# Turning the last attention weights and LayerNorm's sums through DRAM instead of on TensorE, with the late weight loads on ScalarE's queue

## The chip, the cores and the metric

The kernel runs on one core of one Trainium2 chip. A core has five engines, each with its own instruction stream: TensorE (PE, matrix products; its weight loads are shown apart as PEld), VectorE (DVE), ScalarE (ACT), GpSimd (POOL) and SyncE (SP, which here only issues DMAs). They wait for one another through semaphores. An engine works its own stream in order, so an instruction that waits holds everything behind it. The metric is the device time of one execution in microseconds, the median of the runs shown. All arithmetic is in float32, and a matrix product of full precision is built from three passes: each operand is split into a high part (type fp32r) and a low part, and high x high, high x low and low x high are summed.

## The reference, cut to what matters

One layer of a decoder block on 512 tokens of 2048 channels:

```python
h = rms_norm(x); proj = h @ w_in          # split into heads of three mixers
out_a = dilated mixture attention          # 8 heads x 64, windows (128,1), (512,4), (2048,16)
out_b = silu(layer_norm(causal_conv(u * sigmoid(gate))))     # 512 channels, 31 taps
out_c = sliding-window attention with sinks                  # 16 query heads, 2 key heads
x = x + concat(out_a, out_b, out_c) @ w_out
x = x + (silu(h2 @ w_gate) * (h2 @ w_up)) @ w_down,  h2 = rms_norm(x)
```

The A mixer gives, per query, softmax weights over the earlier keys, which the kernel computes as one masked softmax over all 512 tokens. LayerNorm of the B mixer takes mean and variance over its 512 channels for each token.

## The kernel before, in words

Activations lie with channels on the 128 partitions and the 512 tokens along the free dimension. A "slot" is one of 73 SBUF tiles of 128x512. Weights come as units of 128x1024: a DMA into a raw buffer (`pump`, L239 to L251), a cast to the high part on ScalarE (`split_up_to`, L295), a subtraction for the low part on VectorE (L269, `wl`, issued through `lows_now`), then 24 matmuls of 512 columns (L328 to L330). Casts run two units ahead.

The order of everything else is written as ticks. A `Ticks` object holds lists of work due at a tick, and the matmul loops call `tick()` after every six matmuls: eight ticks to an input projection (two units), so ticks 0 to 207 lie in the 26 projections after the head of four, and four to a unit in the first half of the output projection, ticks 208 to 271. `T_MEET = 208` is where the two meet. `late_lows` and `cooling` decide when a unit's subtraction and the next load are issued: in the projections a load follows the release of its buffer by one unit, in the output projection it is issued at the start of the next unit, directly behind the subtraction that read its buffer last, and ahead of the cast of the unit after.

An A head (`attention`, `head`) goes through: scores on TensorE in three units (L863, L864); logits scaled by ScalarE (L941); mask and maximum by VectorE (L946); exponentials by ScalarE (L954, tiles `es[0..2]`); then the weights, which have queries on partitions, must be turned so that keys lie on partitions, as ten 128x128 blocks (causal: 4 + 3 + 2 + 1). Eight of the ten go through DRAM. `blocks_turn` (L971) transposes 32x32 blocks on VectorE into a raw buffer of 128x1024, `blocks_leave` (L976) stores it, `blocks_back` (L983) loads it with the blocks put in place by four DMAs, `blocks_high` (L993) and `blocks_low` (L999) split it into high and low. The other two blocks are turned by TensorE in `flip` (L1006: two transposes into a PSUM bank), then split from PSUM by `high` (L1012) and `low` (L1017). `weigh` (L1030, L1031) multiplies the turned weights with the values.

The depthwise convolution runs as 4 x 31 taps on VectorE (L590), one every 1.4 to 1.9 ticks, with a pause from tick 205 to 215. LayerNorm begins at tick 246 (`T_LN` + 2): `ln_sum`, `ln_split` (L608 to L610), `ln_center` (two matmuls with ones, L617 and L618), `ln_square`, `ln_var` and `ln_out`. `ln_var` turns the sum of squares with four TensorE transposes (`transposed_scale`, L486) and reduces along the free dimension; `ln_out` spreads the result over the partitions with four more (`spread_by_tensor`, L480), at tick 260, and multiplies from PSUM (L633).

In the output projection the product of a unit goes to one of two PSUM banks in turn (pool `tiles`), and VectorE empties the bank with the residual addition (`residual`, L1166, tile `xr`) at the next tick. All DMAs but the first four are issued from SP. Each DMA issue also waits until the DMA that used its completion semaphore before has landed; there are eight such semaphores in turn.

Of the kernel before, what the change touches and what calls it, by code (L numbers as in the profile page):

```python
# [33 lines left out]
OUT_ORDER = (list(range(16)), [n + o for n in range(6) for o in (0, 8)] + [6, 7, 14, 15])  # L34

TAP_TICKS = (1.4, 1.5, 1.9, 1.9)
T_LN = 244
T_MEET = 208
T_GLU = 14

# [20 lines left out]
SPLIT_BUFS = 3  # L61
X_AHEAD = 8
SPLIT_AHEAD = 2
WARM = 8


# [55 lines left out]
def kernel(ctx: ExitStack, tc: tile.TileContext, xT, wi, wo, wgu, wd, cst_in, outT):  # L122
# [118 lines left out]
    def pump(limit, most=99, eng=nc.sync):  # L241
        while at["entry"] < len(entries) and len(raws) < limit and entries[at["entry"]][0] not in held and most:
            most -= 1
            buf, key, parts = entries[at["entry"]]
            size = [part.shape[-1] * (part.shape[1] if len(part.shape) == 3 else 1) for part in parts]
            t, o = take(buf, key, sum(size)), 0
            for part, n in zip(parts, size):
                to = t[:, o:o + n]
                eng.dma_start(to.rearrange("p (n f) -> p n f", n=part.shape[1]) if len(part.shape) == 3 else to, part)
                o += n  # L250
            at["entry"] += 1  # L251

# [221 lines left out]

        ticks.after(2, turn)

    def spread_by_tensor(src4, name):
        b = bank(name)
        for i in range(NT):
            nc.tensor.transpose(b[:, i * P:(i + 1) * P], src4[:, i:i + 1].to_broadcast([P, P]), ident)  # L480
        return b

    def transposed_scale(acc, n, name):
        t, v, r = bank(name), small(name + "v"), small(name + "r")
        for i in range(NT):
            nc.tensor.transpose(t[:, i * P:(i + 1) * P], acc[:, i * P:(i + 1) * P], ident)  # L486
        nc.vector.tensor_reduce(v, t.rearrange("p (a b) -> p a b", b=P), axis=mybir.AxisListType.X, op=ALU.add)
        nc.vector.tensor_scalar(v, v, 1.0 / n, EPS, op0=ALU.mult, op1=ALU.add)
        nc.gpsimd.tensor_tensor(r, v, nhalf[:, :NT], op=ALU.pow)
        return r  # L490

    g4 = [bank(f"in{j}") for j in range(HEAD4)]
    h_hl = {}
    late_lows.append(True)
# [130 lines left out]
            add_square(ln["s"], yconv[j], j, "lq")  # L625

    def ln_var():
        ln["r"] = transposed_scale(ln.pop("s"), 512, "lv")

    def ln_out(mix):  # L630
        b = spread_by_tensor(ln["r"], "lrs")
        for j in range(NB):
            nc.vector.tensor_mul(yconv[j], yconv[j], b)  # L633
        for j in range(NB):
            nc.scalar.activation(yconv[j], yconv[j], AF.Silu, bias=col(C_LB + j), scale=col(C_LG + j))
            mix[f"b{j}"] = yconv[j]
# [179 lines left out]
    def attention(kind, box, mix, mi, heads):  # L816
# [34 lines left out]
        def head(h):  # L851
# [104 lines left out]

            ph, pl = {}, {}

            def block(i, j):
                for u, un in enumerate(us):  # L960
                    for ii, k0, n, o in un:
                        if ii == i:
                            f = o + j * P - k0
                            return es[u][:, f:f + P]

            def blocks_turn():
                z = wp.tile([P, 1024], F32, name=f"{name}z{h}", tag=f"raw{TURN_BUFS[0]}", bufs=1)
                to = z.rearrange("p (j b q) -> p b j q", j=4, b=8)
                for u, c, bs in ((0, slice(0, 2), slice(0, 2)), (0, slice(2, 3), slice(4, 5)), (1, slice(0, 2), slice(2, 6, 3)),
                                 (2, slice(0, 2), slice(3, 7, 3)), (2, slice(3, 4), slice(7, 8))):  # L970
                    nc.vector.transpose(to[:, bs], es[u].rearrange("p (b j q) -> p b j q", b=NT, j=4)[:, c])  # L971
                ticks.after(2, blocks_leave, z)

            def blocks_leave(z):
                d = tc.dram_tile([P, 1024], F32, name=f"{name}ed{h}")
                nc.sync.dma_start(d, z)  # L976
                ticks.after(3, blocks_back, d)

            def blocks_back(d):
                turned[0] = 3 - turned[0]  # L980
                t = wp.tile([P, 1024], F32, name=f"{name}et{h}", tag=f"raw{TURN_BUFS[turned[0]]}", bufs=1)
                for j in range(4):
                    nc.sync.dma_start(t[32 * j:32 * j + 32].rearrange("p (i c) -> p i c", i=4),  # L983
                                      d.rearrange("(i p) c -> p i c", i=4)[:, :, j * 2 * P:(j + 1) * 2 * P])
                ticks.after(5, blocks_high, t.rearrange("p (i b q) -> p b i q", i=4, b=8))

            def queries4(t):
                return t.rearrange("p (b i q) -> p b i q", b=NT, i=4)

            def blocks_high(src):  # L990
                for t in range(2):
                    ph[t] = slot(f"{name}ph{h}{t}", F32R)
                    nc.scalar.copy(queries4(ph[t]), src[:, NT * t:NT * t + NT])  # L993
                ticks.after(EV, blocks_low, src)

            def blocks_low(src):
                for t in range(2):
                    pl[t] = slot(f"{name}pl{h}{t}", F32R)
                    nc.vector.tensor_sub(queries4(pl[t]), src[:, NT * t:NT * t + NT], queries4(ph[t]).bitcast(F32))  # L999

            def flip(t):
                b = bank(f"{name}t{h}{t}")
                o = 0
                for j, i0, i1 in TBANKS[kind][t]:
                    for i in range(i0, i1 + 1):
                        nc.tensor.transpose(b[:, o:o + P], block(i, j), ident)  # L1006
                        o += P
                ticks.after(ev, high, t, b, o)

            def high(t, b, o):  # L1010
                ph[t] = slot(f"{name}ph{h}{t}", F32R)
                nc.scalar.copy(ph[t][:, :o], b[:, :o])  # L1012
                ticks.after(EV, low, t, b, o)

            def low(t, b, o):
                pl[t] = slot(f"{name}pl{h}{t}", F32R)
                nc.vector.tensor_sub(pl[t][:, :o], b[:, :o], ph[t][:, :o].bitcast(F32))  # L1017

            def weigh():
                b = bank(f"{name}o{h}")  # L1020
# [41 lines left out]
            if kind == "c":  # L1062
                ticks.after(tu, packed_exps)
                ticks.after(tu + s2, packed_norm)
                ticks.after(tu + 1, packed_turn)
            else:
                ticks.after(tu + s2, invert, h, den)
                ticks.after(tu + 2, blocks_turn)
                ticks.after(tu + s2 + fl + 2, flip, 2)
            ticks.after(t0 + at_v, weigh)  # L1070
            if h == 1:
                ticks.after(t0 + at_v - 2, sums_back)
# [21 lines left out]
    t_tap = T_GLU + 2  # L1094
    for j in range(NB):
        for i in range(TAPS):
            if T_MEET - 3 <= t_tap < T_MEET + 7:
                t_tap = T_MEET + 7
            ticks.after(int(t_tap), tap, j, i)
            t_tap += TAP_TICKS[j]  # L1100
    t_ln = T_LN
# [3 lines left out]
    ticks.after(t_ln + 4, ln_center)  # L1105
    ticks.after(t_ln + 6, ln_square)
    ticks.after(t_ln + 11, ln_var)
    ticks.after(t_ln + 14, ln_out, mix)
    for n, row in enumerate(r for r in ROWS if r[0] == "b"):
        ticks.after(t_ln + 15 + n, split_mix, row)  # L1110

    shared = {}
    cooling.append(True)
# [679 lines left out]
```

## Time and profile before

| | |
|---|---|
| median of 3 runs | 1826.89 us (1826.79 to 1827.04) |
| the profiled execution | 1827.03 us |
| its span, first to last instruction | 1825.3 us |
| TensorE's granted clock | 0.999 |
| busy PE, DVE, ACT, POOL | 100%, 79%, 73%, 56% |
| DMA traffic | 354.61 MB, mean 194 GB/s |

The profile is one execution. A row of the order of time gives the start and duration in us, the engine, the line of the kernel, the operation, output<-inputs with shapes, a count when alike instructions were merged, and in square brackets the idle time of the engine just before with what ended it. Engine names with q (SPq, ACTq) are the sequencer that issues DMAs. The input projections run from about 9 to 376 us, the output projection to about 562 us, and the feed-forward part takes the rest. The A heads of the four tiles a0 to a3 (two heads each) are turned between about 309 and 434 us.

### The profile page before, as it was taken

How to read it: one execution, taken by the hardware profiler on the slowest of the kernel's cores; microseconds unless marked ns; L12 is line 12 of the kernel's file. 1: busy time of each engine (PE TensorE's matmuls, PEld its weight loads, DVE VectorE, ACT ScalarE, POOL GpSimd, SP SyncE). 2: the span in 40 equal slices, each digit the busy share in tenths (PEclk: the TensorE clock that was granted, in tenths of full speed). 3: DMA queues.
4: the chain of work that ended last, by engine and by line, in shares of the span. 5: the costliest groups of instructions: out<-in, count | busy, mean ns of one | idle time of the engine just before them, and what ended most of it. 6: DMA issues, size and time to landing. Idle time of an engine off the chain costs nothing.

```text
span 1825.3 us, 26570 instructions
## 1 busy us (share of the span) xinstructions
PE 1818.3 (100%) x8191; PEld 1509.9 (83%) x8191; DVE 1434.5 (79%) x1996; ACT 1327.6 (73%) x1848; POOL 1022.1 (56%) x793
## 2 busy tenths in 40 slices
PE   9999999999999999999999999999999999999998
PEld 7888888888888888888888888888888888888887
DVE  6779999987689777777777777777777777777777
ACT  6345656664468778888888888888887778877775
POOL 0116555120014577786887868878775568775652
PEclk9999999999999999999999999999999999999999
DMA  7355456666343557787777877778687579877645
GB/s 279 96 161 157 152 172 182 195 211 214 130 145 113 130 142 206 191 222 192 194 205 191 220 192 197 204 190 223 176 278 261 195 230 293 259 256 255 231 127 105
DMA packets 409295, 354.61 MB, mean 194 GB/s; under 512 B 177088, under 2 KB 331840, under 8 KB 409152
## 3 DMA queue, kind: packets, MB, share of 16 engines
q1 hardware_dynamic: 408576, 352.12, 65.7%
q8 instruction: 65, 1.06, 0.2%
q10 hardware_dynamic: 576, 0.79, 0.1%
q14 instruction: 78, 0.64, 0.1%
HBM read 270.00 MB, written 74.41 MB: 189 GB/s over the span
## 4 chain that ended last, share of the span: by engine, by line
PE 99%; DVE 1%; DMA 0%; issue 0%; ACT 0%; SPq 0%; DVEq 0%; ACTq 0%
PE out L1374 15%; PE out L1375 15%; PE out L1372 15%; PE out L1637 7%; PE out L1639 7%; PE out L1638 7%; PE o L328 3%; PE o L330 3%; PE o L329 3%; PE cq L328 2%; PE cq L329 2%; PE cq L330 2%; PE ak L328 1%; PE aq L328 1%; PE av L328 1%; PE ak L330 1%
## 5 line engine op out<-in xcount | busy, mean ns | idle before, releaser
L1372 PE MATMUL out<-wh,h 128*128 128x512 f32 x1232 | 479.2, 389 | 0.0
L1374 PE MATMUL out<-wl,h 128*128 128x512 f32 x1232 | 479.2, 389 | 0.0
L1375 PE MATMUL out<-wh,h 128*128 128x512 f32 x1232 | 479.2, 389 | 0.0
L1372 PEld LDWEIGHTS out<-wh,h 128*128 128x128 f32 x1232 | 231.2, 188 | 48.1
L1374 PEld LDWEIGHTS out<-wl,h 128*128 128x128 f32 x1232 | 231.2, 188 | 48.1
L1375 PEld LDWEIGHTS out<-wh,h 128*128 128x128 f32 x1232 | 231.2, 188 | 47.9
L1637 PE MATMUL out<-wh,a 128*128 128x512 f32 x620 | 240.4, 388 | 0.0
L1638 PE MATMUL out<-wl,a 128*128 128x512 f32 x620 | 240.3, 388 | 0.0
L1639 PE MATMUL out<-wh,a 128*128 128x512 f32 x620 | 240.3, 388 | 0.0
L295 ACT CAST wh<-w 128x1024 fp32r<-128x1024 f32 (+2 forms) x94 | 97.0, 1032 | 115.8 <-PE o L329 48.9
L1647 DVE TENSOR_TENSOR y<-y,out 128x512 f32<-128x512 f32 x192 | 128.6, 684 | 47.6 <-PE out L1639 46.1
L269 DVE TENSOR_TENSOR wl<-w,wh 128x1024 fp32r<-128x1024 f32 (+2 forms) x95 | 114.1, 1203 | 30.0 <-ACT wh L295 28.9
L1639 PEld LDWEIGHTS out<-wh,a 128*128 128x128 f32 x620 | 116.4, 188 | 24.0
L1638 PEld LDWEIGHTS out<-wl,a 128*128 128x128 f32 x620 | 116.4, 188 | 23.8
L1637 PEld LDWEIGHTS out<-wh,a 128*128 128x128 f32 x620 | 116.4, 188 | 23.8
L590 DVE SCALAR_TENSOR_TENSOR y<-bu,cst,y 128x511 f32<-128x511 f32 (+14 forms) x120 | 89.8, 748 | 0.5
L328 PE MATMUL o<-mh_c,wh 128*128 128x512 f32 x128 | 50.3, 393 | 0.0
L328 PE MATMUL cq<-hh,wh 128*128 128x512 f32 x128 | 50.0, 391 | 0.0
L329 PE MATMUL cq<-hl,wh 128*128 128x512 f32 x128 | 49.9, 390 | 0.0
L329 PE MATMUL o<-ml_c,wh 128*128 128x512 f32 x128 | 49.9, 390 | 0.0
L330 PE MATMUL o<-mh_c,wl 128*128 128x512 f32 x128 | 49.9, 390 | 0.0
L330 PE MATMUL cq<-hh,wl 128*128 128x512 f32 x128 | 49.8, 389 | 0.0
(2359 smaller groups left out, 4736.4 us busy)
## 6 DMA issues: line engine op xcount, KB each, us to landing
od<-a SPq DMA_DIRECT2D x154, 256.0 KB
a<-od SPq DMA_DIRECT2D x154, 256.0 KB
w<-in_wi SPq DMA_DIRECT2D x58, 512.0 KB
w<-in_wo SPq DMA_DIRECT2D x32, 512.0 KB
x<-in_xT SPq DMA_DIRECT2D x16, 256.0 KB
xr<-in_xT SPq DMA_DIRECT2D x16, 256.0 KB
x2d<-xr SPq DMA_DIRECT2D x16, 256.0 KB
z<-x2d SPq DMA_DIRECT2D x64, 64.0 KB
```

The source lines that it names most:

```text
L269: fn(*args)
L295: (nc.vector.tensor_copy if u == 0 else nc.scalar.copy)(hi[:, :n], t[:, :n])
L328: nc.tensor.matmul(out, wh, xh, start=start, stop=False)
L329: nc.tensor.matmul(out, wh, xl, start=False, stop=False)
L330: nc.tensor.matmul(out, wl, xh, start=False, stop=stop)
L1372: nc.tensor.matmul(b, x[:, high], wh[:, s], start=c == f == 0 and q in (7, 1, 5, 2), stop=False, skip_group_check=True)
L1374: nc.tensor.matmul(b, x[:, high], wl[:, s], start=False, stop=False, skip_group_check=True)
L1375: nc.tensor.matmul(b, x[:, low], wh[:, s], start=False, stop=c == f == 1, skip_group_check=True)
L1637: nc.tensor.matmul(b[:, lo:hi], x[:, high], wh[:, s], start=start, stop=False, skip_group_check=True)
L1638: nc.tensor.matmul(b[:, lo:hi], x[:, high], wl[:, s], start=False, stop=False, skip_group_check=True)
L1639: nc.tensor.matmul(b[:, lo:hi], x[:, low], wh[:, s], start=False, stop=last, skip_group_check=True)
L1647: getattr(eng, op)(t, t, src)
```

## The change

Five things are done.

1. `flip`, `high`, `low`, `block` and `queries4` go. `blocks_turn` also transposes, on VectorE, the two blocks that `flip` turned, into a second tile `z2` of 128x256 (a slot); `blocks_leave` stores that too (`ec`), `blocks_back` loads it with four more DMAs (`eu`), and `blocks_high` and `blocks_low` split three tiles where they split two, five ticks after the loads are issued.
2. LayerNorm's `transposed_scale` and `spread_by_tensor` go. `ln_var` calls `token_scale` (a reduction with 32x32 transposes on VectorE, four small DMAs to DRAM one tick later, one back two ticks later, additions and a power on GpSimd three ticks later) and `spread` (a transpose on VectorE two ticks later, four small DMAs, then one that broadcasts the row over 128 partitions into a slot). `ln_out` multiplies from that slot.
3. `T_LN` goes from 244 to 231; the steps up to `ln_var` come 13 ticks sooner, `ln_out` comes at tick 259 in place of 260.
4. The taps' pause ends at tick 211 in place of 215.
5. Weight units with a key of 46 or more (the last 17 units of the input projection and the 32 of the output projection) are loaded by DMAs on ScalarE's queue, at the same points of the program.

```diff
-T_LN = 244
+T_LN = 231
...
+ACT_LOADS = 46
...
-                eng.dma_start(to.rearrange("p (n f) -> p n f", n=part.shape[1]) if len(part.shape) == 3 else to, part)
+                by = nc.scalar if isinstance(key, int) and key >= ACT_LOADS else eng
+                by.dma_start(to.rearrange("p (n f) -> p n f", n=part.shape[1]) if len(part.shape) == 3 else to, part)
...
     def ln_var():
-        ln["r"] = transposed_scale(ln.pop("s"), 512, "lv")
+        ln["r"] = slot("lrs")
+        token_scale(ln.pop("s"), 512, "lv", ticks.after, lambda v, r, wide: spread(wide, "l", ln["r"]))
...
     def ln_out(mix):
-        b = spread_by_tensor(ln["r"], "lrs")
         for j in range(NB):
-            nc.vector.tensor_mul(yconv[j], yconv[j], b)
+            nc.vector.tensor_mul(yconv[j], yconv[j], ln["r"])
...
-                ticks.after(2, blocks_leave, z)
+                z2 = slot(f"{name}z{h}", cols=2 * P)
+                to = z2.rearrange("p (j b q) -> p b j q", j=4, b=2)
+                for n in range(2):
+                    nc.vector.transpose(to[:, n], es[n + 1][:, 2 * P:3 * P].rearrange("p (j q) -> p j q", j=4))
+                es.clear()
+                ticks.after(2, blocks_leave, z, z2)
...
+                d2 = tc.dram_tile([P, 2 * P], F32, name=f"{name}ec{h}")
+                nc.sync.dma_start(d2, z2)
...
+                t2 = slot(f"{name}eu{h}", cols=2 * P)
+                for j in range(4):
+                    nc.sync.dma_start(t2[32 * j:32 * j + 32].rearrange("p (i c) -> p i c", i=4),
+                                      d2.rearrange("(i p) c -> p i c", i=4)[:, :, j * 64:(j + 1) * 64])
...
-                ticks.after(tu + s2 + fl + 2, flip, 2)
...
-            if T_MEET - 3 <= t_tap < T_MEET + 7:
-                t_tap = T_MEET + 7
+            if T_MEET - 3 <= t_tap < T_MEET + 3:
+                t_tap = T_MEET + 3
...
-    ticks.after(t_ln + 14, ln_out, mix)
+    ticks.after(t_ln + 26, ln_out, mix)
     for n, row in enumerate(r for r in ROWS if r[0] == "b"):
-        ticks.after(t_ln + 15 + n, split_mix, row)
+        ticks.after(t_ln + 27 + n, split_mix, row)
```

More of the change, by code (lines that the diff above doesn't have):

```diff
@@ L475, in spread @@
         ticks.after(2, turn)
[L477 to L490, printed above, removed]
     g4 = [bank(f"in{j}") for j in range(HEAD4)]
@@ L957, in head @@
             ph, pl = {}, {}
[L959 to L964, printed above, removed]
             def blocks_turn():
@@ L971, in blocks_turn, with blocks_leave, blocks_back @@
                     nc.vector.transpose(to[:, bs], es[u].rearrange("p (b j q) -> p b j q", b=NT, j=4)[:, c])
-                ticks.after(2, blocks_leave, z)
-            def blocks_leave(z):
+                z2 = slot(f"{name}z{h}", cols=2 * P)
[4 more added lines that the diff above has]
+                ticks.after(2, blocks_leave, z, z2)
+            def blocks_leave(z, z2):
                 d = tc.dram_tile([P, 1024], F32, name=f"{name}ed{h}")
                 nc.sync.dma_start(d, z)
-                ticks.after(3, blocks_back, d)
-            def blocks_back(d):
+                d2 = tc.dram_tile([P, 2 * P], F32, name=f"{name}ec{h}")
+                nc.sync.dma_start(d2, z2)
+                ticks.after(3, blocks_back, d, d2)
+            def blocks_back(d, d2):
                 turned[0] = 3 - turned[0]
@@ L984, in blocks_back @@
                                       d.rearrange("(i p) c -> p i c", i=4)[:, :, j * 2 * P:(j + 1) * 2 * P])
[L985 to L991, printed above, removed]
+                t2 = slot(f"{name}eu{h}", cols=2 * P)
+                for j in range(4):
+                    nc.sync.dma_start(t2[32 * j:32 * j + 32].rearrange("p (i c) -> p i c", i=4),
+                                      d2.rearrange("(i p) c -> p i c", i=4)[:, :, j * 64:(j + 1) * 64])
@@ L992, in blocks_high, with by_query @@
+                b8 = t.rearrange("p (i b q) -> p b i q", i=4, b=8)
+                ticks.after(5, blocks_high, (b8[:, :NT], b8[:, NT:], t2.rearrange("p (i b q) -> p b i q", i=4, b=2)))
+            def by_query(t, src):
+                return t[:, :src.shape[1] * P].rearrange("p (b i q) -> p b i q", i=4, q=32)
+            def blocks_high(srcs):
+                for t, src in enumerate(srcs):
                     ph[t] = slot(f"{name}ph{h}{t}", F32R)
-                    nc.scalar.copy(queries4(ph[t]), src[:, NT * t:NT * t + NT])
@@ L994, in blocks_high, with blocks_low @@
-                ticks.after(EV, blocks_low, src)
-            def blocks_low(src):
-                for t in range(2):
+                    nc.scalar.copy(by_query(ph[t], src), src)
+                ticks.after(EV, blocks_low, srcs)
+            def blocks_low(srcs):
+                for t, src in enumerate(srcs):
                     pl[t] = slot(f"{name}pl{h}{t}", F32R)
[L999 to L1017, printed above, removed]
+                    nc.vector.tensor_sub(by_query(pl[t], src), src, by_query(ph[t], src).bitcast(F32))
             def weigh():
```

## The prediction

> **What bounds the kernel now.** I read the page first (the span, the busy shares, the chain that ended last), then TensorE's waits, then the order of time on each engine around the places that the diff names.
>
> ```profile
> span 1825.3 us, 26570 instructions
> ...
> PE 1818.3 (100%) x8191; PEld 1509.9 (83%) x8191; DVE 1434.5 (79%) x1996; ACT 1327.6 (73%) x1848; POOL 1022.1 (56%) x793
> ...
> PE 99%; DVE 1%; DMA 0%; issue 0%; ACT 0%; SPq 0%; DVEq 0%; ACTq 0%
> ```
>
> The waits of TensorE in the whole execution are two, and both lie outside the part that changes (the start and the last product):
>
> ```profile
> PE idle L354 <- DVE nhalf L360: 1.1, 1, 1.1
> PE sides L1602 <- DVE y L1616: 1.1, 2, 0.6
> ```
>
> So TensorE is the bound, and it never stands still between them. Two things can move the time: TensorE's own instructions that go away, and waits of TensorE that do not exist yet. Everything else is slack, and the question is how much of it there is where the change uses it. The 40 slices of the page cannot show that, since an average over 45 us hides a slack of 1 us. The order of time can.
>
> **What TensorE loses.** Each of the 8 A heads has one `flip`, two 128x128 transposes between two 512-wide matmuls. In the order of time on TensorE:
>
> ```profile
> 315.60 0.40 PE L330 MATMUL ak<-hh,wl 128*128 128x512 f32 x1
> 315.83 0.38 PE L1006 MATMUL a0t<-ident,a0e 128*128 128x128 f32 x2
> 315.97 0.47 PE L328 MATMUL ak<-hh,wh 128*128 128x512 f32 x1
> 316.29 0.39 PE L329 MATMUL ak<-hl,wh 128*128 128x512 f32 x1
> ```
>
> From the start of L330 to the start of L329 two matmuls normally pass, each 0.23 us after the other (315.60 to 315.83). That is 0.46 us, and here it is 0.69: the pair costs 0.23. The chain tells the same, and gives the two groups of four that LayerNorm uses (L486, L480):
>
> ```profile
> 316.00 0.22 PE a0t L1006 x2
> ...
> 454.82 0.44 PE lv L486 x4
> ...
> 459.39 0.44 PE lrs L480 x4
> ```
>
> Eight pairs at 0.23 are 1.84 us, LayerNorm's 0.88, in sum 2.7. The matmuls just behind an interruption start up to 0.01 us late for some steps, which may add some tenths; I take 2.8.
>
> One transpose alone is longer than its place in the queue:
>
> ```profile
> L1006 PE MATMUL a0t<-ident,a0e x4: 270/272/273, 315.8 to 328.4; 128*128 128x128 f32 x4
> ```
>
> If each took its whole 0.272 us out of TensorE's time, 24 would give 6.5 us. That is a rival below; the starts above speak against it. [...]
>
> **What takes the place.** Per head VectorE gets two more 128x128 transposes, ScalarE and VectorE keep one copy and one subtraction each (now from SBUF, five ticks later, with the other two), and SyncE's queue (SP) gets one store and four loads. LayerNorm's variance gets ten small DMAs on SP and a few short instructions on VectorE and GpSimd. In 380 to 440, where A heads 2 and 3 run beside the output projection, VectorE is the busy one; in 382 to 388 it is full:
>
> ```profile
> 382.00:388.00 6.00, 6.00 (x31) 5.08 (x30) 5.97 (x14) 4.14 (x12) 0.00 (x0) 1.00 0.19 39
> ...
> 380.00:440.00 60.00, 60.00 (x285) 50.24 (x284) 48.50 (x105) 34.08 (x72) 2.31 (x3) 1.00 0.69 215
> ```
>
> The columns are the window, its length, then PE, PEld, DVE, ACT, POOL busy (count), clock, DMA share, GB/s. So I look at that place step by step. First SP, which runs there without a pause:
>
> ```profile
> 349.43 0.34 SPq L976 DMA_DIRECT2D a1ed<-a1z  x1
> ...
> 351.10 0.60 SPq L249 DMA_DIRECT2D w<-in_wo  x1
> ...
> 358.16 2.02 SPq L983 DMA_DIRECT2D a1et<-a1ed  x4
> ...
> 364.35 0.58 SPq L249 DMA_DIRECT2D w<-in_wo  x1
> 365.11 0.34 SPq L664 DMA_DIRECT2D aq2t<-aq2d  x1
> 365.50 0.43 SPq L249 DMA_DIRECT2D w<-in_wo  x1
> ```
>
> **SP's term.** A head's new store and four loads cost one issue like L976 and four like L983: 0.34 + 2.02 = 2.4 us in front of aq2t. The two weight loads ahead of aq2t leave: 0.60 + 0.58 = 1.2. Net +1.2 from this head. Of the head before it (another 2.4, less its own loads) pauses of SP take part; bounds 0 to 1.2 more, since nothing that I see gives time back. I take aq2t 1.5 us later, between 0 (if the shorter ring makes the transfers land sooner) and 2.4.
>
> **The path from aq2t to TensorE.** It is short of slack at each step:
>
> ```profile
> 374.33 0.82 ACT L941 ACTIVATE a2s<-a2s,aq2r 128x128 f32<-128x128 f32 x2 [4.06 <-POOL aq2r L674]
> ...
> 383.08 1.05 ACT L295 CAST wh<-w 128x1024 fp32r<-128x1024 f32 x1
> ```
>
> ```profile
> 375.72 0.69 DVE L1086 TENSOR_TENSOR ml_c<-mix_c,mh_c 128x512 fp32r<-128x512 f32 x1 [2.92 <-ACT mh_c L1085]
> ...
> 382.03 0.69 DVE L1086 TENSOR_TENSOR ml_a<-mix_a,mh_a 128x512 fp32r<-128x512 f32 x1 [2.29 <-ACT mh_a L1085]
> ...
> 385.12 1.22 DVE L269 TENSOR_TENSOR wl<-w,wh 128x1024 fp32r<-128x1024 f32 x1
> 386.25 0.68 DVE L1166 TENSOR_TENSOR xr<-xr,o 128x512 f32<-128x512 f32 x1
> 386.94 1.45 DVE L971 STREAM_TRANSPOSE a2z<-a2e 128x256 f32<-128x256 f32 x5
> ...
> 389.02 0.73 DVE L590 SCALAR_TENSOR_TENSOR y<-bu,cst,y 128x490 f32<-128x490 f32 x1
> 389.66 1.22 DVE L269 TENSOR_TENSOR wl<-w,wh 128x1024 fp32r<-128x1024 f32 x1
> ...
> 391.91 0.69 DVE L1166 TENSOR_TENSOR xr<-xr,o 128x512 f32<-128x512 f32 x1
> ```
>
> ```profile
> 387.93 0.39 PE L328 MATMUL o<-mh_c,wh 128*128 128x512 f32 x1
> ...
> 393.82 0.39 PE L328 MATMUL o<-mh_c,wh 128*128 128x512 f32 x1
> ```
>
> ScalarE stood 4.06 us waiting for GpSimd's aq2r (which comes from aq2t), VectorE then 2.92 and 2.29 us for ScalarE, and VectorE's xr (L1166, the residual that empties a PSUM bank) ends at 386.93, while TensorE's third unit of the output projection, which writes that bank again (two banks, in turn), starts at 387.93. The slack is 1.0 us; at the next unit it is 393.82 - 392.60 = 1.2.
>
> Into this path the change puts: 1.5 us of SP; two weight loads that ScalarE now issues where the output projection begins; and two taps, since the pause ends four ticks sooner (tick 211 in place of 215, one tap per 1.9 ticks), ahead of xr. A DMA issue on ScalarE's queue is seen once, at the start, four in 1.86 us:
>
> ```profile
> 0.80 1.86 ACTq L249 DMA_DIRECT2D w<-in_wi  x4
> ```
>
> So the loads cost 0.93 together (0 if they hide behind a running instruction), and a tap 0.64 (389.02 to 389.66), two of them 1.3. TensorE itself arrives 4 x 0.23 = 0.9 sooner. Stall at this bank: 1.5 + 0.9 + 1.3 + 0.9 - 1.0 = 3.6 us; from 0 (nothing on SP, issues hidden, transfers sooner) to 4.5 (SP at 2.4).
>
> **The weight loads as waits on ScalarE.** A load into a buffer waits for the `wl` subtraction that read it last. On SP that wait is seen in 376 to 476:
>
> ```profile
> SPq L249 <- DVE wl L269: 29.5, 8, 10.0
> ```
>
> There only DMAs stand behind it. On ScalarE the next unit's cast, the exponentials, the logits and the copies out of PSUM stand behind it, and VectorE waits for those. At the second unit ScalarE is ready at 383.08, and wl ends at 386.34: it would stand 3.3 us. From E, the end of that wl: issue 0.46, cast 1.05, the last exponential and its sum some 0.9, then a2z 1.45 and two new transposes 0.5 (1.45 / 5 each), that is E + 4.4; from there the rows as before, from the end of a2z (388.39) to the end of the second xr (392.60), 4.2: E + 8.6, where it was E + 6.3. This is 2.3 later against a slack of 1.2: a further 1.1, between 0 (if the issue goes out ahead of a running instruction and VectorE has other work) and 2.3. [...]
>
> Seven more of the eight waits follow, at later units. Their bounds are 0 and about 8 us (the 29.5 scaled by the 3.3 us at the second unit against the longest, 10.0, is 9.7, less the 1.1 used). I take 2.5, near the lower end, because ScalarE has 26 of 60 us free in 380 to 440.
>
> **LayerNorm's mean in TensorE's queue.** It moves 13 ticks forward, into the stretch where heads 3 run.
>
> ```profile
> 439.65 0.69 DVE L610 TENSOR_TENSOR lnl<-lns,lnh 128x512 fp32r<-128x512 f32 x1 [2.77 <-ACT lnh L609]
> ```
>
> ```profile
> 443.63 0.39 PE L618 MATMUL lnm<-lnl,one 128*128 128x512 f32 x1
> ```
>
> TensorE's second matmul of the mean starts 3.3 us after the end of lnl (440.34). VectorE and ScalarE some 3 us late use that up: 0 to 2 us, I take 0.5. The two DRAM trips have 15 ticks of 1.4 us (six matmuls); I cost them at nothing. Their cover is that stretch; were it gone, VectorE's multiplications would wait for the broadcast and the `xr` behind them would be late, which the 8 us above hold.
>
> **Sum.** -2.8 + 3.6 + 1.1 + 2.5 + 0.5 = +4.9 us. The profiled execution took 1827.03 us (1.7 outside its span), the median of the runs is 1826.89, so the difference between them is 0.1 and I let it go: 1827.0 + 4.9 = 1832 us, +0.27%. With all upper ends: -2.8 + 4.5 + 2.3 + 8 + 2 = +14.0, 1841. With all costs at 0: 1824.1. A difference under 0.2%, 3.65 us, cannot be told from none.
>
> **Rivals.**
> - **No stall (not slower).** One mechanism: the smaller ring. With the weight loads on the other queue SP's transfers land sooner, aq2t is not late, and ScalarE's long wait at 374.33 shrinks by as much as taps and issues add. It decides at the bank of 387.93: if xr ends no more than 0.1 us later than now (its 1.0 slack less the 0.9 that TensorE comes sooner), there is no wait, and the time is 1827.0 - 2.8 = 1824.2, within 0.2%. For it: ScalarE has waits to give. Against: VectorE has none in 382 to 388.
> - **The stall stays at two banks.** VectorE catches up in 400 to 440. Then -2.8 + 3.6 + 1.1 = +1.9, 1829, within 0.2%.
> - **The transposes cost their whole duration**: 24 x 0.272 = 6.5 without stalls, 1820.5, faster. Against it stand the starts at 315.83 to 316.29. [...]
> - **The waits go whole to ScalarE and on to TensorE**: 29.5 - 2.8, 1854. Against: TensorE has over 1 us in most units.
>
> **How the numbers follow.** The forecast case 0.47 (1830.5 to 1841), no stall 0.25, two banks 0.17, whole durations 0.06, whole waits 0.05. Faster by over 0.2% is 0.06, within 0.25 + 0.17 = 0.42, slower 0.47 + 0.05 = 0.52. The range runs from 1823.8 (no stall, some tenths better) to 1841.5 (the upper ends) and leaves out the two smallest cases.
>
> **What would show it.** Right: no L1006, L486 or L480 on TensorE and 24 fewer matmuls and 24 fewer weight loads; TensorE waits for VectorE's L1166 rows (xr) near 387 and 393, in sum 3 to 9 us; ScalarE waits for wl at its weight loads; aq2t issued 1 to 2 us later on SP. Wrong: no waits of TensorE in 370 to 480 and a span 2.8 shorter (the slack was larger than the bank rows say), or TensorE waits first on a weigh or a score (then SP's lag, not VectorE, decides).

## The result, and the profile after

| | before | after |
|---|---|---|
| median of 4 runs, us | 1826.84 (1826.44 to 1827.04) | 1846.16 (1842.84 to 1848.08) |
| ratio, 95% interval | | 1.0104 (1.0087 to 1.0122) |
| the profiled execution, us | 1827.03 | 1848.08 |
| its span, us | 1825.3 | 1846.4 |

The change makes the kernel 19.3 us slower. The prediction was 1832.0 with a range to 1841.5: the direction was right, the size was not. Line numbers below are those of the kernel after the change where its profile is read (the residual xr is L1139, the cast L297, the weight load L251, the low part wl L271).

The page of after, its head and its chain of waits:

```profile
span 1846.4 us, 26614 instructions
...
PE 1824.0 (99%) x8167; PEld 1512.0 (82%) x8167; DVE 1438.3 (78%) x2013; ACT 1327.0 (72%) x1848; POOL 1026.3 (56%) x796
...
PE 73%; DVE 1%; issue 0%; DMA 0%; ACT 0%; DVEq 0%
```

TensorE has its 24 matmuls fewer (8191 to 8167), and yet more busy time. TensorE's waits in the whole execution (total, times, longest in us):

```profile
PE a2s L850 <- DMA aq<-aq2l: 8.9, 1, 8.9
PE o L330 <- ACT mh_b L1058: 3.0, 1, 3.0
PE o L330 <- DVE xr L1139: 1.8, 3, 1.3
...
PE a1o L1004 <- ACT a1ph L985: 1.0, 1, 1.0
PE lnm L604 <- DVE one L595: 0.6, 1, 0.6
PE a1o L1005 <- DVE a1pl L991: 0.2, 1, 0.2
PE lnm L605 <- DVE lnl L597: 0.2, 1, 0.2
```

Where there were no waits in the changed part, there are 15.7 us now. The largest is the first score of A tile 2 (L850), which waits for a DMA that copies the low part of its queries to the other half of the partitions (aq<-aq2l, issued at L689 and L690). I call these two DMAs the twin copies. The second is put down to mh_b, a row of mixer B, since a cast of such a row was the last thing to end before it. But the matmul that stood there, at 482.30, belongs to the first half of the output projection, which reads rows of mixer C only; the first matmul with mh_b starts at 497.5. VectorE's xr ended 0.15 us before that matmul started, as another did 0.14 us before the one at 407.63, so this wait too is one for xr. With it the waits for xr, which the prediction put first, are 4.8 us, none of them near 387 or 393.

The waits are not all. The stretches with the two long ones, before and then after (window, length, busy PE, PEld, DVE, ACT, POOL with counts, clock, DMA share, GB/s):

```profile
376.00:388.00 12.00, 12.00 (x57) 10.06 (x56) 9.59 (x23) 10.07 (x24) 1.04 (x1) 1.00 0.52 163
476.00:492.00 16.00, 16.00 (x72) 13.24 (x71) 7.66 (x12) 5.53 (x9) 0.00 (x0) 1.00 0.37 131
```

```profile
376.00:388.00 12.00, 8.31 (x29) 7.19 (x30) 6.69 (x11) 5.33 (x11) 4.24 (x3) 0.59 0.83 235
476.00:492.00 16.00, 12.97 (x45) 10.15 (x44) 8.91 (x12) 5.99 (x9) 0.00 (x0) 0.79 0.29 98
```

The granted clock was 1.00 and is 0.59 and 0.79. In the order of time on TensorE, behind the two waits:

```profile
379.69 0.45 PE L850 MATMUL a2s<-ak2h,aq 128*128 128x128 f32 x1 [8.87 <-DMA aq<-aq2l]
...
381.11 0.63 PE L331 MATMUL aq<-hl,wh 128*128 128x512 f32 x1
381.54 0.63 PE L332 MATMUL aq<-hh,wl 128*128 128x512 f32 x1
...
482.30 0.76 PE L330 MATMUL o<-mh_c,wh 128*128 128x512 f32 x1 [3.03 <-ACT mh_b L1058]
...
488.38 0.40 PE L332 MATMUL o<-mh_c,wl 128*128 128x512 f32 x1
```

A step of 512 columns takes 0.43 us there (381.11 to 381.54) in place of 0.23. From 482.30 to 488.38 lie 14 steps, 6.1 us in place of 3.2: 2.9 us lost. From 379.69 to 385.99 TensorE does matmuls of 6912 columns in sum, 6.3 us where 13.5 steps of 0.23 are 3.1: 3.2 lost. So the account of the profiled execution is 15.7 of waits + 6.1 of slow clock - 2.8 of transposes = 19.0; the spans differ by 21.1. Most of the other 2 us lies at the edges of the nine waits. A row's idle time begins at the end of the matmul before, 0.39 us after its start, where without a wait the next one starts after 0.23; so each wait costs 0.16 us more than its row says, 1.4 in sum, and the first step behind a wait is some 0.1 longer than others (0.56 us from 482.30, where the next ones take 0.43).

Why the twin copies are late is seen on SP, after:

```profile
351.07 4.28 SPq L974 DMA_DIRECT2D a1eu<-a1ec  x4
...
370.51 2.38 SPq L970 DMA_DIRECT2D a1et<-a1ed  x4
...
377.26 0.47 SPq L689 DMA_DIRECT2D aq<-aq2l  x1
377.77 0.60 SPq L690 DMA_DIRECT2D aq<-aq2l  x1
378.87 0.34 SPq L651 DMA_DIRECT2D aq2t<-aq2d  x1
```

aq2t was issued at 365.11 before; it is 13.8 us later, where the prediction had 1.5. And why xr is late before 482.30, on VectorE and ScalarE:

```profile
472.60 2.49 DVE L620 TENSOR_TENSOR y<-y,lrs 128x512 f32<-128x512 f32 x4 [2.17 <-DMA lrs<-le]
...
476.17 0.60 ACT L1058 CAST mh_a<-mix_a 128x512 fp32r<-128x512 f32 x1
478.71 0.34 ACTq L251 DMA_DIRECT2D w<-in_wo  x1
479.14 1.04 ACT L297 CAST wh<-w 128x1024 fp32r<-128x1024 f32 x1 [2.37 <-PE o L331]
480.09 2.17 ACT L1058 CAST mh_b<-y 128x512 fp32r<-128x512 f32 x4
...
480.74 0.69 DVE L1059 TENSOR_TENSOR ml_b<-y,mh_b 128x512 fp32r<-128x512 f32 x1 [2.10 <-ACT mh_b L1058]
481.46 0.69 DVE L1139 TENSOR_TENSOR xr<-xr,o 128x512 f32<-128x512 f32 x1
```

VectorE first stands 2.17 us for LayerNorm's broadcast (lrs). ScalarE, free at 476.77, stands in front of the weight load until 478.7, when VectorE's wl has ended (L271, from 477.41, 1.22 long). The cast of the weights behind that load (wh) is put down to a matmul of TensorE that ended at 479.04, as late as the load's issue, so the load is not the only thing in front of it. Then come the casts of the b rows; VectorE stands 2.10 us for the first of them, and xr is behind that.

### The profile page after: what moved, and what is told of

The parts are those of the page before. It is cut to its first block, busy times and chain, and to the rows that moved or that the text cites. A ratio compares the mean times of both kernels' runs of the same rounds, so it can differ in the third digit from the quotient of the medians.

```text
span 1846.4 us, 26614 instructions
## 1 busy us (share of the span) xinstructions
PE 1824.0 (99%) x8167; PEld 1512.0 (82%) x8167; DVE 1438.3 (78%) x2013; ACT 1327.0 (72%) x1848; POOL 1026.3 (56%) x796
## 4 chain that ended last, share of the span: by engine, by line
PE 73%; DVE 1%; issue 0%; DMA 0%; ACT 0%; DVEq 0%
PE out L1347 15%; PE out L1345 15%; PE out L1348 15%; PE out L1610 7%; PE out L1612 7%; PE out L1611 7%; PE o L330 2%; PE o L331 2%; PE o L332 2%; DVE wl L293 0%; DVE y L1620 0%; DMA out_T<-z 0%; DVE z L1519 0%; ACT mh_b L1058 0%; DVE y L1589 0%
## 5 line engine op out<-in xcount | busy, mean ns | idle before, releaser
L297 ACT CAST wh<-w 128x1024 fp32r<-128x1024 f32 (+2 forms) x94 | 96.9, 1031 | 133.9 <-PE o L331 43.7
L271 DVE TENSOR_TENSOR wl<-w,wh 128x1024 fp32r<-128x1024 f32 (+2 forms) x95 | 114.1, 1203 | 28.2 <-ACT wh L297 23.8
```

The lines of the kernel that those rows point to most:

```text
L271: fn(*args)
L297: (nc.vector.tensor_copy if u == 0 else nc.scalar.copy)(hi[:, :n], t[:, :n])
```

## The experiments

The theories were these. **V** is the prediction's: SP a little late, then VectorE and ScalarE too tight at the banks of the first output units. **S**: the added issues on SP. **Q**: the weight loads on ScalarE's queue, whatever else. Later ones are named where they come up. All ratios are against the kernel before, measured beside it on the same chip. "Twin" is the issue of the first aq<-aq2l on SP and TensorE's wait for it, in the profiled execution (363.20 and none before).

| run | ratio, 95% interval | twin issued, wait (us) |
|---|---|---|
| after | 1.0104 (1.0087 to 1.0122) | 377.26, 8.9 |
| e1 loads back on SP | 1.0063 (1.0048 to 1.0078) | 367.78, 2.3 |
| e2 only loads on ScalarE | 1.0081 (1.0065 to 1.0096) | 367.65, 0.9 |
| e3 only the turn | 1.0020 (1.0010 to 1.0029) | 370.95, 2.6 |
| e4 only LayerNorm, taps | 1.0040 (1.0025 to 1.0055) | 361.64, 0 |
| e5 as e4, sums on TensorE | 1.0020 (1.0011 to 1.0029) | 363.36, 0 |
| e6 as e4, 4 ticks sooner | 1.0015 (1.0005 to 1.0024) | 364.43, 0 |
| e7 loads of 46 to 62 only | 1.0000 (0.9990 to 1.0009) | 367.24, 0 |
| e8 as e2, a unit later | 1.0022 (1.0013 to 1.0031) | 368.11, 1.0 |
| e9 LayerNorm at old ticks | 1.0007 (0.9997 to 1.0016) | 360.92, 0 |
| e11 after, a unit later | 1.0072 (1.0055 to 1.0089) | 373.11, 7.6 |
| e12 as e1, 5 loads on ScalarE | 1.0080 (1.0065 to 1.0095) | 372.47, 6.2 |
| e14 as e3, DMAs on GpSimd | 0.9989 (0.9980 to 0.9999) | 362.41, 0 |
| e15 as e1, 5 loads on GpSimd | 1.0076 (1.0061 to 1.0091) | 373.35, 6.8 |
| e16 all, repaired | 0.9993 (0.9984 to 1.0002) | 364.78, 0 |
| e17 e14 again | 0.9991 (0.9982 to 1.0000) | 367.19, 1.0 |
| e18 as e1, 3 loads on GpSimd | 1.0062 (1.0040 to 1.0085) | 370.12, 3.3 |
| e19 as e1, 3 loads on ScalarE | 1.0066 (1.0044 to 1.0089) | 371.10, 5.1 |
| e20 after, turn on GpSimd | 1.0092 (1.0075 to 1.0109) | 368.73, 2.9 |

e14 and e17 are one kernel: its twin came at 362.41 in one execution and at 367.19 in another. A difference of a few us in that column alone proves little; groups of runs do.

### The parts by themselves

e1 undoes the weight loads; e2, e3 and e4 are the kernel before with one part each.

```diff
-ACT_LOADS = 46
+ACT_LOADS = 999
```

> The change with one part undone: the weight loads from unit 46 on are issued by SP again. Theory Q (the loads on ScalarE's queue are the cause: ScalarE stands before each of them, and SP, which shares the eight completion semaphores with it, is held too): the wait of 8.9 us for aq<-aq2l and the slow clock behind it go, and so does most of the wait for mh_b; 1825 to 1831 us. Theory S (the turn's and LayerNorm's extra issues on SP are the cause, whoever issues the loads): SP now has the weight loads as well, so the wait stays or grows; 1840 us or more. Theory V (my prediction's: VectorE and ScalarE too tight at the banks of the first output units): 1828 to 1832, with waits for xr.

> The kernel before with one part of the change alone: weight loads from unit 46 on by ScalarE's queue. Theory Q: most of the loss shows without the rest, 1834 to 1846 us, with ScalarE idle 3 to 6 us ahead of loads in 340 to 390 and SP's aq2t several us later than 365.1. Theory S: within 2 us of the kernel before, 1825 to 1829. Theory V: 1827 to 1831 (0.9 us of issues and waits for wl on ScalarE).

> The kernel before with one part alone: all ten blocks of every A head turned through DRAM (one more store and four more loads per head on SP), the rest as before. Theory Q: TensorE loses 1.8 us of transposes, small waits come; 1824 to 1830 us. Theory S: SP's 2.4 us per head add up (8 heads), aq2 late by 5 us or more, TensorE waits at aq<-aq2l; 1834 us or more. Theory V: 1826 to 1829 (SP 1.5 to 2.4 us later, slack of 1 us at the bank of 387.93).

> The kernel before with one part alone: LayerNorm's variance through DRAM trips with T_LN 231 and the taps' pause ending at 211. All theories of the first loss (Q, S, V): TensorE loses eight transposes (0.9 us), 1825.5 to 1827 us. If the trips themselves make the b rows late (my prediction cost them at nothing): TensorE waits for mh_b by about 3 us, and 1829 to 1833 us.

Measured, in us against 1826.5 of before: e1 1837.98 (+11.5), e2 1841.74 (+15.2), e3 1830.02 (+3.5), e4 1833.41 (+6.9). So no theory of one cause stands: every part costs something alone, and they add up to 25.6, more than the 19.3 of all together. e4, which all three theories had near 1826, is the plainest miss; the reading beside them, that the trips cost, is met in kind (1833.41 against 1829 to 1833), but with a wait for xr and not for mh_b. The profiled execution of e2 is the fastest of its four (1837.97), that of e3 the slowest of its ten (1834.42), so their waits are not those of the medians. TensorE's waits, of e1, e2, e3 and e4:

```profile
PE o L330 <- DVE xr L1139: 7.3, 3, 5.1
PE a2s L850 <- DMA aq<-aq2l: 2.3, 1, 2.3
```

```profile
PE o L330 <- DVE xr L1168: 9.5, 4, 3.6
...
PE a2s L865 <- DMA aq<-aq2l: 0.9, 1, 0.9
```

```profile
PE a2s L863 <- DMA aq<-aq2l: 2.6, 1, 2.6
PE o L328 <- DVE xr L1152: 2.5, 1, 2.5
```

```profile
PE o L328 <- DVE xr L1151: 4.4, 1, 4.4
```

The prediction's waits for xr are there, in e2 above all, where they are 9.5 us.

### The weight loads on ScalarE's queue

ScalarE's idle time in e2, between 376 and 485, by what ended it:

```profile
ACT wh L297 <- DVE wl L271: 22.0, 7, 5.8
ACT wh L297 <- issue: 20.1, 7, 3.6
```

```profile
396.41 0.34 ACTq L251 DMA_DIRECT2D w<-in_wo  x1
396.79 1.05 ACT L297 CAST wh<-w 128x1024 fp32r<-128x1024 f32 x1 [3.29 <-DVE wl L271]
```

42.1 us of ScalarE stand in front of a load, and the cast behind it starts 0.4 us after it is issued. Two runs test whether it is the wait for wl (theory **W**) or the queue as such (theory **C**: ScalarE and SP share eight completion semaphores, in the trace of after 214 DMAs of the two to each). e7 moves only the loads of the projections, which come one unit after their buffer is released; e8 moves all, but issues those of the output projection one unit later.

```diff
+                by = nc.scalar if isinstance(key, int) and ACT_LOADS <= key < 63 else eng
```

```diff
         if late_lows and not cooling:
-            pump(RAW_EARLY if at["use"] <= 20 else RAW_BUFS)
+            n = room(RAW_BUFS) if at["use"] > 2 * N_IN + 1 else 0
+            if n:
+                due.append(n)
...
         at["use"] += 1
+        if due:
+            pump(RAW_BUFS, due.pop())
```

> The kernel before with the weight loads of units 46 to 62 alone on ScalarE's queue (the projections, where a load comes one unit after its buffer is released); the 32 of the output projection stay on SP. Theory W (what costs is a load's wait for the subtraction wl, placed ahead of the next cast): those loads have nothing to wait for, so 1826 to 1829 us. Theory C (the eight completion semaphores that the two queues share hold both, wherever the loads are): ScalarE idle before these loads too, 1832 us or more.

> The run with the loads from 46 on by ScalarE's queue alone, with each load of the output projection issued one unit later in ScalarE's stream, when the subtraction that read its buffer is long done. Theory W: ScalarE's 42 us of waits ahead of casts in 376 to 485 fall under 15, TensorE's waits for xr go; 1826 to 1830 us. Theory C: they stay for the most part, 1835 us or more.

e7: 1826.90, no difference. e8: 1831.21, a little over W's range; of e2's 15.2 us 10.7 are gone, no cast of e8 waits for wl any more, and TensorE's waits for xr fell from 9.5 to 0.6:

```profile
PE a2s L880 <- DMA aq<-aq2l: 1.0, 1, 1.0
PE o L345 <- DVE xr L1183: 0.6, 1, 0.6
```

W is shown, as the larger part of the loads' price. What stays in e8, 4.5 us by the medians, is only 1.6 in waits of its profiled execution (1829.29 us, under the median of its runs), and the twin copies are 4 to 5 us later than before in the profiled executions of e2, e7 and e8 alike, though SP has fewer issues there. W does not explain that.

### LayerNorm

VectorE in e4 at the place of the 4.4 us:

```profile
461.13 2.50 DVE L618 TENSOR_TENSOR y<-y,lrs 128x512 f32<-128x512 f32 x4 [4.35 <-DMA lrs<-le]
...
467.79 0.69 DVE L1151 TENSOR_TENSOR xr<-xr,o 128x512 f32<-128x512 f32 x1
```

It stands 4.35 us for the broadcast (lrs<-le), and the xr that empties TensorE's bank is behind. Theory **T** says that the two DRAM trips are not covered, theory **O** that ln_out at tick 259 and the shorter pause are too tight whatever turns the sums.

> The run with LayerNorm and the taps alone, but its sums again turned on TensorE (eight transposes back): T_LN 231, ln_out at tick 259, the taps' pause to 211. Theory T (the DRAM trips are later than tick 259 lets them be): without them 1825.5 to 1828.5 us, no wait for xr near 468. Theory O (the earlier tick and the shorter pause make VectorE too full where A head 3 is turned, whatever turns the sums): 1832 us or more, the wait near 468 stays.

> The run with LayerNorm and the taps alone, its steps up to the variance four ticks (5.6 us) sooner (T_LN 227), ln_out and the b rows at the same ticks as there. Theory T: the 4.35 us that VectorE stood for the broadcast are covered, TensorE's wait for xr near 468 goes; 1825.5 to 1828 us. Theory O: the wait stays or moves to the mean's two matmuls (lnm); 1831 us or more.

e5 1830.62, e6 1829.25: each lies between the two, so each theory has a part. In e5 a wait of 1.9 us for xr stays near 466 with no trip at all, in e6 one of 2.5; and 0.3 and 0.8 us near 388, where the pause is shorter. e9 takes O's part away and gives the trips three ticks more (18 in place of 15).

```diff
-T_LN = 231
+T_LN = 229
...
-            if T_MEET - 3 <= t_tap < T_MEET + 3:
-                t_tap = T_MEET + 3
+            if T_MEET - 3 <= t_tap < T_MEET + 7:
+                t_tap = T_MEET + 7
...
-    ticks.after(t_ln + 26, ln_out, mix)
+    ticks.after(t_ln + 29, ln_out, mix)
```

> LayerNorm's variance through DRAM alone, with nothing else made tighter: T_LN 229 (two ticks sooner than in the change), ln_out and the b rows at tick 260 and 261 as in the kernel before, the taps' pause to 215 as before. If what the earlier runs showed is all (trips that were not covered; ln_out one tick sooner, ahead of an xr; two taps more ahead of the xr near 388), no wait is left and TensorE is 0.9 us shorter: 1825.5 to 1826.5 us. If the trips as such cost (SP's ten issues): 1828 us or more.

1827.96, between the two ranges and not told apart from before by its interval: the waits near 388 and 466 are gone, but one of 2.7 us has come at 447. VectorE's longest wait in e9 in 430 to 450:

```profile
DVE lvv L452 <- POOL lvv L451: 8.5, 1, 8.5
```

The program waits for the first trip's return three ticks after the tick of its load. VectorE stands 8.5 us at that short instruction (L452), and the next xr is behind it. So a trip is short of cover at both its ends, and more time at the second does not help the first.

### The turn on SP

The prediction priced the turn by SP's time. e14 leaves the turn as in e3 and issues its five new DMAs of each head from GpSimd.

```diff
-                nc.sync.dma_start(d2, z2)
+                nc.gpsimd.dma_start(d2, z2)
...
-                    nc.sync.dma_start(t2[32 * j:32 * j + 32]
+                    nc.gpsimd.dma_start(t2[32 * j:32 * j + 32]
```

> The turn alone, with its five new DMAs of each head (one store, four loads) on GpSimd's queue in place of SP's. Theory S2 (SP has no pause from one A head to the next, so each head's five issues add up): aq<-aq2l is issued near 363 as before (370.95 with them on SP), its wait of 2.6 us goes; 1824.5 to 1827.5 us. If the transfers and not the issues are late (more traffic on the 16 engines): the wait stays at 2 us or more; 1829 us or more.

> The turn alone with its five new DMAs per head on GpSimd's queue, once more, for the interval: 1824.0 to 1825.5 us if the 1.84 us of TensorE's transposes are gained whole but for small waits; 1826 or more if the first result was luck.

1824.67 and, measured again, 1825.42: in place of +3.5 us the turn now gives 2.3 and 1.4 us, and both are faster than before by no more than a little. GpSimd, where the four loads of a head take 2.2 us, had nothing urgent there:

```profile
354.43 2.18 POOL L987 DMA_DIRECT2D a1eu<-a1ec  x4 [3.62 <-DMA a1ec<-a1z]
```

So the turn's whole loss was its place on SP, 4.9 to 5.8 us (3.5 lost there against 1.4 and 2.3 gained here). The transfers are the same in e3 and e14. e14 does not tell apart SP's time for the issues and its waits for completion semaphores (in the traces of before and after, every one of 1654 and 1704 issues ends 0.28 us or more after the landing of the DMA that had its semaphore before).

### The wait for the twin copies

The turn alone gave 2.6 us, the loads on ScalarE's queue 0.9, the whole change 8.9. e11 is the whole change with e8's edit, e12 is e1 with five loads on ScalarE's queue (units 63 to 67, issued in 337 to 373).

```diff
+                by = nc.scalar if isinstance(key, int) and 63 <= key < 68 else eng
```

> The whole change, with the loads of the output projection issued one unit later in ScalarE's stream. The waits for wl go, so the waits for xr at 407, 447 and 455 go and LayerNorm's casts are not held at 478. Theory C (the 8.9 us for aq<-aq2l come from ScalarE's and SP's queues holding one another through the shared completion semaphores in 340 to 377, where these loads have no wait for wl): that wait stays, 1838 to 1843 us. Theory W (all of the loss on ScalarE's queue is the wait for wl): the wait falls to 2 or 3 us as with the loads on SP, 1830 to 1836 us.

> The run with all loads back on SP, but for five: units 63 to 67, which are issued in 340 to 378, go on ScalarE's queue. Theory C: these five make most of the 8.9 us; aq<-aq2l is issued at 373 or later (367.8 with all on SP) and TensorE waits 5 to 9 us there; 1843 us or more. Theory W: their buffers are long free, so nothing changes or SP gains their five issues; 1835 to 1839 us.

e11 1839.79 with a wait of 7.6 us, e12 1841.57 with 6.2. By the wait that is C's side: five loads that wait for no wl seem enough, though e12's time lies between the two ranges. But C named the shared semaphores, and e15 puts those five on GpSimd's queue, away from ScalarE's stream.

> The run with five loads (units 63 to 67) on ScalarE's queue, those five on GpSimd's queue instead, whose DMAs have completion semaphores of their own. Theory C (ScalarE's stream and the eight semaphores that SP and ScalarE share): aq<-aq2l is issued at 368 or sooner (372.5 with ScalarE, 367.8 with SP), TensorE waits 2.5 us or less there; 1834 to 1839 us. Theory B (a second queue's 512 KB transfers take the 16 engines from SP's, whoever issues them): 371 or later, a wait of 4 us or more; 1840 us or more.

1839.91, and the wait is 6.8 us: that is B's side, and C falls, as far as the semaphores and ScalarE go (in e15's program the five loads have five semaphores that no other DMA of it uses). In e15 GpSimd issues the five at 332.2, 342.3, 354.1 (two) and 359.6; in e1 SP issues them at 340.2, 349.4, 355.6 and then, behind the twin copies, at 368.9 and 370.1. Theory **D**: two loads of 512 KB overtake. e18 and e19 leave those two on SP.

```diff
-                by = nc.gpsimd if isinstance(key, int) and 63 <= key < 68 else eng
+                by = nc.gpsimd if isinstance(key, int) and 63 <= key < 66 else eng
```

> Five loads (units 63 to 67) on GpSimd's queue made aq<-aq2l wait 6.8 us (2.3 with all on SP). Here 63 to 65 alone are on GpSimd's queue; 66 and 67 are on SP, where they stand behind aq<-aq2l. Theory D (off SP's queue the loads of 66 and 67 go out ahead of aq<-aq2l and of the DMAs before it, and take the 16 engines from them): aq<-aq2l issued at 366 to 369 us, a wait of 1 to 3 us, 1833 to 1838 us. Theory Q2 (any load on a second queue holds SP's small DMAs, however placed): 371 or later, a wait of 4 us or more, 1839 us or more.

> The same with ScalarE's queue: 63 to 65 on ScalarE, 66 and 67 on SP (with all five on ScalarE: aq<-aq2l at 372.5 us, a wait of 6.2 us, 1841.6 us). Theory D: 366 to 369 us, a wait of 1 to 3 us, 1835 to 1839 us. Theory C (ScalarE's in-order stream and the eight completion semaphores that it shares with SP): three loads still hold both, 371 or later, a wait of 4 us or more, 1839 us or more.

1838.38 and 1840.19, with waits of 3.3 and 5.1 us (e1 2.3, e12 6.2, e15 6.8). e18 lies between what D and Q2 expected; e19 meets its rival's figures (C: 371.10, 5.1 us, 1840.19), though e15 spoke against that rival. With a spread of 4.8 us between executions of one kernel the two do not settle the shares, and their ratios do not differ from e1's by more than the intervals. Rows of e12 speak against D there:

```profile
306.17 3.27 SPq L646 DMA_DIRECT2D aq1d<-aq1p  x4
...
355.69 1.35 SPq L823 DMA_DIRECT2D a1sums<-weights_sums  x4
```

In e1 the same two are issued at 304.29 and 351.26. So e12 is 1.9 us late before the first of its five loads goes out (at 337.3), where both kernels still do the same, and 4.4 of the 4.7 us are there before the first of the two that D names (364.4); the other one, at 373.0, is behind the twin copies. In e15 the rows agree with D: SP is 0.7 us behind e1 at 357 and 3.4 at 363, just after GpSimd's last load. The last run takes the turn's DMAs off SP in the whole change.

> The whole change, weight loads on ScalarE's queue included, with the turn's five new DMAs per head on GpSimd's queue. If SP's 40 added issues are what lets the wait for aq<-aq2l grow to 8.9 us: it falls to 0 to 2 us (0.9 with the loads on ScalarE's queue alone), and with it the slow clock behind it; what stays are the waits for xr, b rows and casts, 1832 to 1839 us. If the loads on the other queue are enough by themselves once LayerNorm and the taps are moved: a wait of 5 us or more, 1841 us or more.

The wait fell from 8.9 to 2.9, a little over what was expected, but the time only to 1843.26, outside the expectation. TensorE's waits in e20, and the row behind the longest for xr in the order of time:

```profile
PE o L330 <- DVE xr L1139: 5.7, 3, 4.2
PE o L330 <- ACT mh_b L1058: 4.9, 1, 4.9
PE a2s L850 <- DMA aq<-aq2l: 2.9, 1, 2.9
```

```profile
394.07 0.77 PE L330 MATMUL o<-mh_c,wh 128*128 128x512 f32 x1 [4.19 <-DVE xr L1139]
```

The wait of 4.9 us, put down to mh_b, is again one for xr, which ended 0.15 us before the matmul at 477.14 started. A wait of 4.2 us for xr has come at 394. In the change it was not seen: there TensorE was 9 us late from the twin copies, which gave VectorE the time. This is one reason why the parts add up to more than the whole.

What the profiled executions show: with the turn's issues on SP and five or more loads on another queue the wait was 6 to 9 us in four runs of four (after, e11, e12, e15); with one of the two back it was 0 to 3 us (e1, e2, e3, e7, e8, e20). What is not settled: how the loads on another queue delay SP's chain of trips, and how much of it is the two that overtake.

### The change without its waits

e16 has all 24 transposes away, the turn as in e14, loads on SP, LayerNorm as in e9 with three ticks more for the first trip.

```diff
-            after(3, power, t)
+            after(landing, power, t)
...
+        token_scale(ln.pop("s"), 512, "lv", ticks.after, lambda v, r, wide: spread(wide, "l", ln["r"]), 6)
```

> The aim of the change with its found costs taken out: all A blocks turned through DRAM with the five new DMAs per head on GpSimd's queue, LayerNorm's variance through DRAM with T_LN 229, three ticks more for its first trip, ln_out at tick 260 and the pause to 215 as before, weight loads on SP. 24 transposes fewer on TensorE are 2.8 us; a wait of 1.0 us for the cast near 388 was left with the turn alone. Theory (the added waits were all of the loss): 1823.0 to 1825.5 us. Rival (LayerNorm's ten DMAs in SP's full stream cost by themselves): 1827 us or more.

1824.88: 1.9 us under before, not told apart from none by its interval. In its profiled execution the added waits are 0.6 us (at the twin copies of a C head), and the span is 2.8 us shorter:

```profile
span 1822.5 us, 26660 instructions
...
PE 1815.4 (100%) x8167; PEld 1508.1 (83%) x8167; DVE 1436.1 (79%) x2013; ACT 1327.5 (73%) x1848; POOL 1045.4 (57%) x836
```

## Why the prediction was right and wrong

- **What TensorE loses, 2.8 us: right to some tenths.** e16 shows a span 2.8 us shorter with 0.6 of waits, and 2.9 us less busy time. The rival of whole durations (6.5 us) falls.
- **SP's term: the step that failed first.** The prediction said "I take aq2t 1.5 us later, between 0 [...] and 2.4". It counted the DMAs of one head and a part of the next. Four heads (two each of a0 and a1) stand ahead of aq2t on SP, 4 x 2.4 = 9.6 us of issues, and SP's pauses took little of them. Those over 0.2 us are 14.8 us in sum from 309 to 347 of before, where SP stands for data (5.3 us for a0ed alone), and 1.9 us from 347 to aq2t. The turn alone made it 7.8 us later (365.11 to 372.87 in e3, in the slowest of its executions), the whole change 13.8. The 1.2 us credited for the two loads that leave did not show, nor the sooner landings of the rival without a stall: with loads on another queue the twin copies came 4 to 5 us later, not sooner, and aq2t at 368.96, 369.15 and 369.43 (e2, e7, e8), though executions of one kernel differ by as much.
- **The path from aq2t to TensorE: a real path, the wrong stop.** The term of 3.6 us was put at the bank of 387.93. TensorE's first long stop was at 370.8, at the score, for the twin copies, which are issued on the same queue just ahead of aq2t. The prediction named this as its own refutation: "or TensorE waits first on a weigh or a score (then SP's lag, not VectorE, decides)". It waited first on a weigh (1.0 and 0.2 us), then on the score (8.9). The bank's wait was covered by that; e2 (2.3 us at 391) and e20 (4.2 at 394) show it where the score waits less, and in both ScalarE stands longer for aq2r than before (5.7 and 5.8 us, 4.06 before).
- **The weight loads as waits on ScalarE: right in kind, too small.** 1.1 + 2.5 us were taken, with 0 to 10.3 as bounds. Alone they gave 9.5 us of waits for xr (e2), and 0.6 once the wait for wl was out of the way (e8). In the change all waits for xr are 4.8 us, and 3.0 of them have LayerNorm's trips in front.
- **LayerNorm's mean: right.** 0.5 us taken, 0.8 measured (lnm).
- **LayerNorm's trips, "I cost them at nothing": wrong.** Alone 4.4 us and the slow clock behind it (e4). In the change it is the wait of 3.0 us at 482.30, with VectorE's 2.17 us for the broadcast and a load's wait for wl in front (above); e11, where no load waits for wl, still has 2.4 us for xr there. The 15 ticks are the whole way; what counts is the four ticks at its end and the three at its first landing, and VectorE stands at each with an xr behind (e4, e9).
- **The clock: missing.** No term was there for TensorE's own slowness after a wait, 6.1 us of the profiled execution.

In sum the terms of the waits were 7.7 us. What they named, xr and the mean, came to 5.6, near the forecast by luck, since the xr waits lie elsewhere and 3.0 us of them stand behind the trips priced at nothing. What the sum did not have is the 10.1 us at the weigh and the score and the 6.1 of clock. So the direction was right, but not for the reason given.

## What to carry to other kernels

When a queue has few pauses ahead of the critical transfer (here 1.9 us in the last 18), most of what a change adds to it there counts (here up to 7.8 of 9.6 us): add up all issues from the last pause on, not those of the last step, and look at every transfer of the queue near the critical one. An instruction that waits costs what is queued behind it on its engine: in before and after, the instructions of VectorE, GpSimd and SP and, its DMA issues apart, ScalarE start in the order of the program. So a load goes where its wait has ended (9.5 us of waits for xr in e2, 0.6 in e8), and a trip through DRAM needs cover at each place where an engine stands for it (4.35 us in e4, 8.5 in e9). A wait also hides the next one (the 4.2 us at 394 in e20), so parts measured singly do not add up (25.6 us against 19.3), and a wait that goes may only uncover another.

## What was not expected of the hardware

- **The clock after a short wait.** The granted clock fell to about half (0.50 in 482 to 486 of after) behind all 12 waits of TensorE over 4 us in these runs, behind 6 of the 16 from 1.8 to 3.6 us, and behind none of the four of 1.3 to 1.4. Windows of e1 (wait of 2.3 us at 370) and e20 (4.2 us at 394), then of e2 (3.6 us at 480), columns busy PE, clock, DMA share, GB/s:

```profile
370.00:374.00 4.00, 3.87 (x13) 0.61 0.92 224
```

```profile
394.00:398.00 4.00, 3.93 (x11) 0.58 0.93 343
```

```profile
480.00:484.00 4.00, 3.85 (x17) 1.00 0.41 134
```

  A step of 512 columns takes 0.43 us at the slow clock (after, 381.11 to 381.54) and 0.23 otherwise. From 1.8 to 3.6 us the length of the wait does not decide it alone: 2.3 us in e1 were enough, 3.6 us in e2 were not. What else decides is not shown. Whether this also makes the times spread is not shown either: runs of e1 to e4 spread over 3.3 to 6.3 us and the 13 of the kernel before beside them over 2.7, but those of e16, whose profiled execution has hardly a wait, over 7.1.
- **Loads taken off a full queue did not make it sooner.** In e7 SP has 17 issues fewer, and the twin copies came at 367.24, not 363.20; in e15, with five loads on GpSimd's queue, at 373.35 for 367.78. These are single executions: e17, with all loads on SP, had them at 367.19 too. No run here shows the reason.
